# A planned layer kernel: row-tile loads planned longer, and the next block's norm roots formed beside the streams and spread through DRAM

## The chip, the cores and the metric

The kernel runs on one core of a Trainium2 chip. The metric is the device time of one execution in microseconds (us); the times shown for the kernel before are from three runs. The engines are named as in the profile: PE (TensorE, with PEld for its weight loads), DVE (VectorE), ACT (ScalarE), POOL (GpSimd) and SP (SyncE, which here only issues transfers). ScalarE issues some transfers too; that queue is written ACTq.

## The reference

One decoder layer on x of 2048 rows by 1024 columns, float32. In short:

```
h = x * rsqrt(mean(x*x, axis=-1) + 1e-6) * norm_g
p = h @ w_in                       # 7552 columns, split into three branches and gates
y_a = rwkv7(p_r, p_k, p_v, p_w, p_a) * silu(z_a)      # recurrence, 8 heads x 64
y_b = sliding_window_attention(p_q, p_sk, p_sv) * silu(z_b)   # window 128, rotary, sinks
y_c = cross_attention(p_xq, mem) * silu(z_c)          # 4 heads x 128, 256 memory rows
merged = sum over i of sigmoid(gate_i) * (y_i @ w_proj_i)
out = x + merged @ w_out
```

What the change touches is the first line: every row of x has one factor, the root of its mean square to the power -1/2. The kernel needs h transposed (channels on partitions, rows of x along the free axis), so the 512 factors of a block must stand in a tile of 128 x 512 in which all partitions hold the same row.

## The kernel before, in words

**Blocks.** The 2048 rows are worked in four blocks of 512 (`for sb in range(nsb)`, L1400). The block's h lies in SBUF as two tiles `hH`, `hL` of 128 x 8 x 512: each float32 value is split into a high part in a shorter format and the rest. A product of two such pairs takes three matmuls (high-high, high-low, low-high: L534, L535, L536 in `gemm3`). Weights come from DRAM, are split by ScalarE and VectorE (L515, L516) into tiles `whl` and put back to DRAM once (`k`, L520); later blocks fetch the split pair (L511).

**Streams.** Within a block, two generators are woven: `stream_r` prepares and runs the recurrence in 8 chunk steps (`rwkv_chain`), `stream_f` does cross attention, window attention, merges and gates. Each `yield` is an estimate of its work in us, `PACE` scales it, and `weave` always advances the generator whose clock is lowest. That gives the program order. A third generator, `x_sums` (L1354), sums the squares of the next block's x: eight times it yields 45, loads a 128 x 512 piece of x on ACTq into the one tile `sx` (L1360), and squares it on ScalarE with a running sum into `ss` (L1362).

**The end of a block.** When all streams are through, the recurrence's outputs are split, `rope_tables(sb + 1)` builds the next rotary tables (a load of the positions, spread to all partitions, then VectorE), and `x_scales` (L1364) makes the factors: VectorE adds the two halves of `ss` (L1370), GpSimd scales and takes the power -1/2 (`rpow`, L489 and L491), giving `rs` of 128 x 4. Then `bcast_T` spreads them: VectorE repeats each column 128 times (L572), TensorE transposes four 128 x 128 tiles into a PSUM tile `as_` (L574), and ScalarE copies that into `rb` (L1375). Next comes `merge(0, ...)`, which adds the first branch into the accumulators (L1321, L1322, L1328), then `x_cols` (L1378): eight loads of x transposed on ACTq (L1384), each multiplied by `rb` on VectorE (L1387) and split into `hH` (L1389, ScalarE) and `hL` (L1390, VectorE). Last, `output` multiplies by `w_out` (L1338 to L1340) and adds x (L1345).

**Row tiles.** `tmp()` and `rt_()` take tiles named `rt` from a ring of six. The temporaries of the rotary tables, the repeated roots, `rb` and the `xt` pieces all come from it, in program order.

**The planner.** The program order is not what the engines run. `steps` gives each instruction a rank (its place in the program, moved for some kinds), and `lay_out` simulates all engines: at each moment an engine takes, of the instructions that are ready by its clock, the one with the lowest rank. Tiles of a ring are opened in program order. The order found is then fixed for each engine (`order`). Engines run in that order whatever the real times are: an instruction that is not ready holds all that stand behind it on its engine. Costs are in `cost_PE` and so on. For a transfer the planner adds:

```
self.dur, self.busy = 4200 if parked else 2200, 420          # L144, ns
self.late = 5000 if any(r[0].startswith("sx") for r in self.writes) else 0
...
wires = s.end = max(wires, s.end) + s.bytes / 380
s.end += s.late
```

So a load of 256 KB counts 2.2 us and 0.69 us; the `sx` loads count 5 us more.

Of the kernel before, what the change touches and what calls it, by code (L numbers as in the profile page):

```python
# [9 lines left out]
F32 = mybir.dt.float32  # L10
# [10 lines left out]
TB = 512  # L21
# [30 lines left out]

LAT = {"PE": 200, "DVE": 45, "ACT": 35, "POOL": 80, "SP": 30}
NAMES = {mybir.EngineType.PE: "PE", mybir.EngineType.DVE: "DVE", mybir.EngineType.Activation: "ACT",
         mybir.EngineType.Pool: "POOL", mybir.EngineType.SP: "SP"}
# [2 lines left out]
class Step:  # L60


    def __init__(self, ins, masks):
        self.ins, self.eng = ins, NAMES[ins.engine]
        self.reads, self.writes = ([self.region(a.bass_ap, masks) for a in aps if getattr(a, "bass_ap", None) is not None]
                                   for aps in (ins.ins, ins.outs))
        self.reads, self.writes = ([r for r in l if r] for l in (self.reads, self.writes))
        self.before, self.after, self.opens, self.group, self.end, self.next = set(), [], [], [], None, None
        self.lat = LAT[self.eng]
        self.chain = self.eng == "PE" and any(r[0].startswith(("Zt", "W_", "R_")) or r[0] in ("W", "R") for r in self.reads)  # L70
        if self.eng == "PE":
            self.lat = 600
        outs = [a.bass_ap for l in (ins.outs, ins.ins) for a in l if getattr(a, "bass_ap", None) is not None]
        rows = [a.offset // math.prod(list(a.tensor.shape)[1:]) for a in outs[:1] + [a.bass_ap for a in ins.ins if getattr(a, "bass_ap", None) is not None]]
        self.rows = rows[0], max(rows)
        self.bytes = 512 * self.n((self.writes + self.reads)[0]) if self.is_dma() else 0
        getattr(self, "cost_" + ("SP" if self.bytes else self.eng))()

    def is_dma(self):
# [62 lines left out]
    def cost_SP(self):  # L142
        parked = any(r[0].startswith(("fq", "fb", "fv", "fn", "fy")) for r in self.reads + self.writes)
        self.dur, self.busy = 4200 if parked else 2200, 420  # L144
        self.late = 5000 if any(r[0].startswith("sx") for r in self.writes) else 0


def steps(instructions, manual, groups, follow, ahead=1000):

    out, masks, seen, byname, opener = [], {}, {}, {}, {}  # L150
    for ins in instructions:
        if isinstance(ins, mybir.BassTilePoolBoundary):
            continue
        s = Step(ins, masks)
        for rs, w in ((s.reads, False), (s.writes, True)):
            for name, parts, words, _, psum, _ in rs:
                s.before |= {q for q, w2, p2, m2 in seen.get(name, ()) if (w or w2 or psum) and q is not s and p2 & parts and m2 & words}
        for name, parts, words, *_ in s.reads:
            seen.setdefault(name, []).append((s, False, parts, words))
        for name, parts, words, *_ in s.writes:  # L160
            old = seen.setdefault(name, [])
            old[:] = [x for x in old if x[0] is s or x[2] & ~parts or x[3] & ~words] + [(s, True, parts, words)]
        s.before |= {byname[x] for x in manual.get(ins.name, ())}
        s.before |= {opener.setdefault(r[0], s) for r in s.writes + s.reads} - {s}
        for b in s.before:
            b.after.append(s)
        byname[ins.name] = s
        s.rank = len(out)
        if any(r[0].startswith(("whl", "raw")) and (s.bytes or r[5] == F32R) for r in s.writes):
            s.rank = max(s.rank - ahead, min(s.rank, FRONT))  # L170
        if s.eng != "PE" and any(r[4] for r in s.reads):
            s.rank -= 600 + 1000 * any(r[0].startswith("mm_") for r in s.reads)
        if s.eng == "DVE" and s.writes and s.writes[0][0].startswith(("ibc", "Yi")):
            s.rank += 500
        out.append(s)
    for a, b in follow.items():
        byname[a].next = byname[b]
    for names in groups:
        group = [byname[n] for n in names]
        group[0].group = group[1:]  # L180
        needs = set().union(*(s.before for s in group)) - set(group)
        for s in group:
            for b in needs - s.before:
                b.after.append(s)
            s.before |= needs
    return out
# [132 lines left out]
def build(tc, A, nsb=4):  # L319
# [30 lines left out]
    def s_ps():  # L350
        return ps.tile([128, 512], F32, name="as_", bufs=2)
# [1002 lines left out]
    def x_sums(sb, ss):  # L1354

        for i in range(4):
            for u in range(2):
                yield 45
                xr = gp_.tile([128, 512], F32, name="sx", bufs=1)
                load = nc.scalar.dma_start(xr, A["x"][sb * TB + i * 128:sb * TB + (i + 1) * 128, u * 512:(u + 1) * 512])  # L1360
                manual[load.ins.name] = [newest[0]]
                S.activation(xr, xr, AF.Square, accum_out=ss[:, i, u:u + 1])  # L1362

    def x_scales(sb, ss=None):  # L1364

        if not sb:
            rs = row_sums(x0)
        else:
            rs = xp.tile([128, 4], F32, name="rs", bufs=2)
            V.tensor_tensor(rs, ss[:, :, 0], ss[:, :, 1], op=ALU.add)  # L1370
        rpow(rs, rs, EPS, 1.0 / D)
        bc = s_ps()
        bcast_T(bc, rs, 1, 4)
        rb = tmp()
        S.activation(rb, bc, AF.Copy)  # L1375
        return rb
# [23 lines left out]
    for sb in range(nsb):  # L1400
        wa = proj(B_WA, hT)
        low = shift(wa, B_WA, pcol("mu_wa"), dcol("omu_wa"), sb, "rr_")
        S.activation(low[EV], low[EV], AF.Tanh)

        lwla = [rp.tile([128, TB], F32R, name=f"lwla{i}") for i in range(2)]
        for t, h, o in zip(lwla, (EV, OD), (OD, EV)):
            S.activation(t[h], low[h], AF.Copy)
            V.tensor_tensor(t[o], low[h], t[h].bitcast(F32), op=ALU.subtract)
        yas = []
        ya, yb, yc_ = ([], []), ([], []), ([], [])  # L1410
        accs = []

        def stream_r():
            parks = park(sb)
            dk = xp.tile([128, 4, NC_], F32, name="dk", bufs=1)
            Pl = xp.tile([128, 4, NC_], F32, name="Pl", bufs=1)
            yts = []
            for p0 in (0, 2):
                group = []
                fn, fy = (dp.tile([4, 2, NC_, 32, 32], F32, name=f"{n}{sb}_{p0}") for n in ("fn", "fy"))  # L1420
                for p in (p0, p0 + 1):
                    yield from rwkv_prep(p, p - p0, parks, dk, Pl, fn, sb, hT, lwla, group)
                yield from rwkv_inverse(group, parks, fn, fy)
                yts += [g[2] for g in group]
            yield from rwkv_chain(parks, dk, Pl, hT, yts, yas)
            yield 0.412

        def stream_f():
            for h in range(4):
                yield from cross_head(h, sb, hT, *yc_)  # L1430
            if not sb:
                rope_tables(0)
            yield from swa_kv(sb, hT)
            yield 6.938
            for j in range(4):
                yield from weave(swa_pair(j, sb, hT, *yb), merge(2, *yc_, accs, hT, first=True, orange=(2 * j, 2 * j + 1)))
            yield from merge(1, *yb, accs, hT)
            for o in range(8):
                gates.append(gate(0, o, hT))
                yield 5.908  # L1440

        gates = []
        ss = xp.tile([128, 4, 2], F32, name="ss", bufs=2)
        streams = [paced(g, PACE[min(sb, 1)][i]) for i, g in enumerate((stream_r(), stream_f()))]
        if sb + 1 < nsb:
            streams.append(x_sums(sb + 1, ss))
        for _ in weave(*streams):
            pass
        for p in range(4):
            split_y(yas[p], *ya, "a", p, sb)  # L1450
        rb = None
        if sb + 1 < nsb:
            rope_tables(sb + 1)
            rb = x_scales(sb + 1, ss)
        parts = []
        for o in range(8):
            for _ in merge(0, *ya, accs, hT, gates=gates, orange=(o,)):
                pass
            parts.append(split_acc(accs[o]))
        if rb is not None:  # L1460
            hT = x_cols(sb + 1, rb)
        output(sb, *zip(*parts))
# [4 lines left out]
def paced(g, paces):  # L1467

    for f, d in zip(paces, g):
        yield f * d  # L1470
# [83 lines left out]
```

## Time and profile before

| | |
|---|---|
| median of three runs | 2141.29 us (2141.21 to 2143.42) |
| profiled execution | 2142.16 us, its span 2140.3 us |
| granted TensorE clock | 1.0 |
| ACT busy | 803.4 us of the span |
| POOL busy | 140.5 us |
| moved by DMA | 519.17 MB, mean 243 GB/s |
| first and last issue of the 24 `sx` loads | 103.5 and 1550.5 us |

How to read it: the profile is one execution, recorded by the hardware. A row of the timeline has the start in us from the span's start, the duration in us, engine, line, operation, the tile written and the tiles read, the shape, and in brackets how long the engine had been idle and what ended that. A row of a group has the count and, for one tile, the durations of the shortest, the median and the longest in ns. Matmuls are pipelined, so that their spans overlap, and what one costs is read from the starts. The ends of the blocks, where the change works, lie at about 500 to 580, 1000 to 1090 and 1520 to 1610 us. The last block has no next x.

### The profile page before, as it was taken

The numbers are of one execution on the slowest core, as the hardware profiler recorded it, in microseconds if no ns is written. First come the engines' busy times: TensorE is split into PE (matmuls) and PEld (weight loads), VectorE is DVE, ScalarE is ACT, GpSimd is POOL, SyncE is SP. The second block draws the span as 40 slices with busy tenths as digits, with TensorE's granted clock in tenths as the row PEclk, the third lists the DMA queues.
The fourth block names the chain that finished last, engine by engine and source line by source line (L and its number), as shares of the span: only waits on it lengthen the run. The fifth ranks groups of instructions, "written<-read, shape, count | busy, mean of one in ns | idle before, by whom it ended". The sixth has DMA issues, their size and how long they took to land.

```text
span 2140.3 us, 37430 instructions
## 1 busy us (share of the span) xinstructions
PE 2124.0 (99%) x14248; PEld 1750.1 (82%) x14248; DVE 1429.2 (67%) x3246; ACT 803.4 (38%) x1699; POOL 140.5 (7%) x180
## 2 busy tenths in 40 slices
PE   9999999999999999999999999999999999999999
PEld 7888788778888888878788888887888888888787
DVE  7879888568477777546647778736455777873532
ACT  7655555335343343313424434410423334331220
POOL 1001000001001000001001000000100010000000
PEclk9999999999999999999999999999999999999999
DMA  9987898988876678695877667877676666768665
GB/s 333 361 284 266 275 300 273 348 297 263 277 213 200 189 218 233 199 313 189 278 255 216 199 178 229 235 235 256 214 265 215 210 196 203 230 188 273 209 207 180
DMA packets 308594, 519.17 MB, mean 243 GB/s; under 512 B 89280, under 2 KB 175552, under 8 KB 308416
## 3 DMA queue, kind: packets, MB, share of 16 engines
q1 hardware_dynamic: 292288, 487.42, 71.4%
q10 hardware_dynamic: 16128, 29.37, 4.2%
q8 instruction: 113, 1.85, 0.4%
q14 instruction: 65, 0.53, 0.1%
HBM read 378.80 MB, written 137.89 MB: 241 GB/s over the span
## 4 chain that ended last, share of the span: by engine, by line
PE 90%; DVE 4%; DMA 3%; issue 1%; ACT 1%; SPq 0%; POOL 0%; ACTq 0%; DVEq 0%
PE mm L535 22%; PE mm L534 22%; PE mm L536 22%; PE mm L1338 1%; PE mm L1340 1%; PE mm L1339 1%; PE rw L999 1%; PE rw L1016 1%; PE oo L1287 1%; PE rw L831 1%; DVE whl L516 1%; PE rw L850 1%; PE oo L831 1%; DMA raw<-in_w_in 1%; PE rw L921 0%
## 5 line engine op out<-in xcount | busy, mean ns | idle before, releaser
L534 PE MATMUL mm<-hH,whl 128*128 128x512 f32 x1888 | 743.6, 394 | 0.4 <-DVE carry L742 0.4
L535 PE MATMUL mm<-hL,whl 128*128 128x512 f32 x1888 | 743.7, 394 | 0.2 <-DVE hL L1390 0.2
L536 PE MATMUL mm<-hH,whl 128*128 128x512 f32 x1888 | 742.1, 393 | 0.0
L534 PEld LDWEIGHTS mm<-hH,whl 128*128 128x128 f32 x1888 | 354.8, 188 | 71.3 <-ACT big L851 0.7
L535 PEld LDWEIGHTS mm<-hL,whl 128*128 128x128 f32 x1888 | 354.9, 188 | 71.2 <-DVE hL L1390 0.6
L536 PEld LDWEIGHTS mm<-hH,whl 128*128 128x128 f32 x1888 | 354.8, 188 | 70.8
L515 ACT ACTIVATE whl<-raw 128x512 fp32r<-128x512 f32 x174 | 108.9, 628 | 124.8 <-PE mm L536 85.4
L516 DVE TENSOR_TENSOR whl<-raw,whl 128x512 fp32r<-128x512 f32 x174 | 119.9, 691 | 50.2 <-ACT whl L515 48.2
L534 PE MATMUL mm<-yh,whl 128*128 128x512 f32 x384 | 151.0, 393 | 0.1
L535 PE MATMUL mm<-yl,whl 128*128 128x512 f32 x384 | 150.2, 391 | 0.0
L536 PE MATMUL mm<-yh,whl 128*128 128x512 f32 x384 | 150.2, 391 | 0.0
L1306 ACT ACTIVATE gt<-mm 128x512 f32<-128x512 f32 x64 | 38.0, 593 | 216.7 <-PE mm L536 216.5
L534 PEld LDWEIGHTS mm<-yh,whl 128*128 128x128 f32 x384 | 72.1, 188 | 15.7 <-ACT gt L1306 0.5
L535 PEld LDWEIGHTS mm<-yl,whl 128*128 128x128 f32 x384 | 72.1, 188 | 14.9 <-DVE yl L1065 0.3
L536 PEld LDWEIGHTS mm<-yh,whl 128*128 128x128 f32 x384 | 72.1, 188 | 14.8
L1321 DVE SCALAR_TENSOR_TENSOR gt<-gt,mm 128x512 f32<-128x512 f32 x32 | 22.0, 687 | 92.3 <-PE mm L536 92.1
L487 POOL TENSOR_SCALAR st<-st 128x4 f32<-128x4 f32 (+1 forms) x32 | 12.5, 391 | 1004.9 <-DVE st L1219 407.4
L1345 DVE SCALAR_TENSOR_TENSOR ya<-mm,ya 128x512 f32<-128x512 f32 x16 | 11.0, 689 | 94.7 <-PE mm L1340 94.7
L1255 ACT ACTIVATE g<-g,mxs,st 128x128 f32<-128x128 f32 x128 | 61.6, 483 | 26.6 <-DVE mxs L1248 26.6
L892 DVE TENSOR_TENSOR ibc<-km,Yi 128x126 f32<-128x126 f32 (+22 forms) x248 | 62.8, 253 | 6.2 <-DMA km<-fn 0.6
L893 DVE TENSOR_TENSOR Yi<-Yi,ibc 128x126 f32<-128x126 f32 (+22 forms) x248 | 62.9, 254 | 5.5
L491 POOL TENSOR_TENSOR st<-st,mhalf 128x8 f32<-128x8 f32 (+1 forms) x36 | 56.2, 1562 | 3.0
(1807 smaller groups left out, 3586.0 us busy)
## 6 DMA issues: line engine op xcount, KB each, us to landing
whl<-k SPq DMA_DIRECT2D x474, 512.0 KB, 4.1
k<-whl SPq DMA_DIRECT2D x162, 512.0 KB, 4.7
raw<-in_w_in SPq DMA_DIRECT2D x118, 256.0 KB, 4.1
fq<-big SPq DMA_DIRECT2D x64, 256.0 KB, 4.5
fb<-big SPq DMA_DIRECT2D x64, 256.0 KB, 4.7
big<-fq SPq DMA_DIRECT2D x32, 512.0 KB, 6.4
big<-fb SPq DMA_DIRECT2D x32, 512.0 KB, 5.6
ya<-in_x ACTq DMA_DIRECT2D x32, 256.0 KB, 5.5
```

The source lines that it names most:

```text
L491: G.tensor_tensor(out, out, mhalf[:, :n], op=ALU.pow)
L515: S.activation(w[:, 0], raw, AF.Copy)
L516: V.tensor_tensor(w[:, 1], raw, w[:, 0].bitcast(F32), op=ALU.subtract)
L534: PE.matmul(out, lh, rh, start=i == 0, stop=False)
L535: PE.matmul(out, lh, rl, start=False, stop=False)
L536: newest[0] = PE.matmul(out, ll, rh, start=False, stop=i == n - 1).ins.name
L831: m = PE.matmul(g[:, c], BK[h, c0 + c], Q[h, c0 + c], start=True, stop=True)
L892: V.tensor_tensor(bc[:, :m, :w], Nb[:, s, s + 1:].unsqueeze(1).to_broadcast([128, m, w]), B[:, :m, s:s + 1].to_broadcast([128, m, w]), op= ...
L893: V.tensor_tensor(B[:, :m, s + 1:], B[:, :m, s + 1:], bc[:, :m, :w], op=ALU.add)
L1255: S.activation(P_, P_, AF.Exp, scale=r2[:, b, i:i + 1], bias=mx[:, b, i:i + 1], accum_out=mx[:, b, 2 + i:3 + i])
L1306: S.activation(t, gp, AF.Tanh, scale=0.5)
L1321: V.scalar_tensor_tensor(g, g, 1.0, pp, op0=ALU.add, op1=ALU.mult)
```

## The change

1. A table `LATE` gives extra landing time by the first letters of the written tile's name: `sx` 5000 ns as before, `rt` 3500 (new), `xr` 6000 (new). It is set to 0 for steps with a rank under 3000.
2. `x_sums` yields 36 in place of 45.
3. `x_scales` is called at the end of a third stream, `stream_x`, right after the sums, and not after all the streams.
4. For blocks after the first, `x_scales` no longer spreads the roots by transposes. It writes `rs` (128 x 4) to a DRAM row `xr` of 512 values with a DMA on SP; its elements go out one by one, since the row runs along the partitions. After the rope tables a second DMA on SP reads that row into all 128 partitions of `rb`. The first block's roots are spread as before.

```diff
+LATE = {"sx": 5000, "rt": 3500, "xr": 6000}
...
+        self.late = next((t for n, t in LATE.items() for r in self.writes if r[0].startswith(n)), 0)
...
-        self.late = 5000 if any(r[0].startswith("sx") for r in self.writes) else 0
...
         s.rank = len(out)
+        if s.rank < 3000:
+            s.late = 0
...
-                yield 45
+                yield 36
                 xr = gp_.tile([128, 512], F32, name="sx", bufs=1)
...
         rpow(rs, rs, EPS, 1.0 / D)
+        if sb:
+            row = dp.tile([1, TB], F32, name=f"xr{sb}")
+            nc.sync.dma_start(row[0].rearrange("(i t) -> t i", t=128), rs)
+            return row
         bc = s_ps()
...
+        rows = []
+
+        def stream_x():
+            yield from x_sums(sb + 1, ss)
+            rows.append(x_scales(sb + 1, ss))
+
         if sb + 1 < nsb:
-            streams.append(x_sums(sb + 1, ss))
+            streams.append(stream_x())
...
             rope_tables(sb + 1)
-            rb = x_scales(sb + 1, ss)
+            rb = tmp()
+            nc.sync.dma_start(rb, rows[0].to_broadcast([128, TB]))
```

## The prediction

> **What bounds the kernel now.** I read the page first: its span and the engines' shares.
>
> ```profile
> span 2140.3 us, 37430 instructions
> PE 2124.0 (99%) x14248; PEld 1750.1 (82%) x14248; DVE 1429.2 (67%) x3246; ACT 803.4 (38%) x1699; POOL 140.5 (7%) x180
> ```
>
> TensorE sets the time. Busy spans of pipelined matmuls overlap, so I took the beat from the starts in the timeline. At the end of block 0 (TensorE's rows) it is this:
>
> ```profile
> 518.76 0.39 PE L534 MATMUL mm<-yh,whl 128*128 128x512 f32 x1
> 518.99 0.39 PE L535 MATMUL mm<-yl,whl 128*128 128x512 f32 x1
> 519.21 0.39 PE L536 MATMUL mm<-yh,whl 128*128 128x512 f32 x1
> 519.88 0.66 PE L574 MATMUL as__5914<-c_ident,rt 128*128 128x128 f32 x4 [0.28 <-DVE rt L572]
> 520.29 0.47 PE L534 MATMUL mm<-yh,whl 128*128 128x512 f32 x1
> 520.61 0.39 PE L535 MATMUL mm<-yl,whl 128*128 128x512 f32 x1
> ```
>
> A 128x512 matmul that lasts 0.39 us is followed by the next after 0.22 to 0.23 us. I take 0.23 for the beat; what is longer than that between two starts is lost or is other work. Only two things can shorten the run: TensorE instructions that go, and beats that are missed. Everything on VectorE, ScalarE, GpSimd and the queues counts only where it makes a beat late. So I looked for the beats that are missed where the change works, at the ends of blocks, and next for what it may spoil elsewhere.
>
> **Removed: the spreading on TensorE.** At the end of blocks 0, 1 and 2 the old `x_scales` repeats the roots over 512 columns on VectorE (L572), transposes four 128x128 tiles (L574) and copies them out on ScalarE (L1375). The other two ends, again TensorE's rows:
>
> ```profile
> 1040.69 0.39 PE L535 MATMUL mm<-yl,whl 128*128 128x512 f32 x1
> 1040.92 0.60 PE L574 MATMUL as__11183<-c_ident,rt 128*128 128x128 f32 x4
> 1041.27 0.48 PE L536 MATMUL mm<-yh,whl 128*128 128x512 f32 x1
> 1041.59 0.40 PE L534 MATMUL mm<-yh,whl 128*128 128x512 f32 x1
> ...
> 1562.98 0.39 PE L536 MATMUL mm<-yh,whl 128*128 128x512 f32 x1
> 1563.21 0.60 PE L574 MATMUL as__16416<-c_ident,rt 128*128 128x128 f32 x4
> 1563.56 0.48 PE L534 MATMUL mm<-yh,whl 128*128 128x512 f32 x1
> 1563.88 0.39 PE L535 MATMUL mm<-yl,whl 128*128 128x512 f32 x1
> ```
>
> In block 0 the three starts 519.21, 520.29, 520.61 span 1.40 us where two beats take 0.46: 0.94 us lost, the wait of 0.28 for L572 within it. In block 1, 1040.69 to 1041.59 is 0.90, so 0.44 lost; in block 2, 1562.98 to 1563.88 is 0.90, again 0.44. Together 1.82 us, which go with certainty, because no instruction of TensorE takes their place. The copies of VectorE and ScalarE that go as well I count at nothing: at these places the matmuls beside them keep their beat.
>
> **Planned longer: loads into row tiles.** The planner (`lay_out`) fixes each engine's order with 2.2 us plus bytes/380 for such a load, 2.2 + 0.69 = 2.9 us for 256 KB. The change adds 3.5 us for tiles named `rt`, so 6.4 us. What loads take, from the DMA issues, issue to landing (the last two rows for what comes below):
>
> ```profile
> rt<-in_xt ACTq DMA_DIRECT2D x24, 256.0 KB, 5.5
> rt<-in_positions SPq DMA_DIRECT2D x4, 256.0 KB, 4.2
> fn<-big SPq DMA_DIRECT2D x64, 32.0 KB, 4.0
> c_bones<-in_bones SPq DMA_DIRECT2D x1, 1.0 KB, 5.0
> ```
>
> 5.5 us against a plan of 2.9: VectorE comes to the product with `xt` (L1387) too early and, being in order, holds what stands behind it. At the end of block 1 that reaches TensorE. Timeline, from the ACT queue's, VectorE's and TensorE's rows:
>
> ```profile
> 1043.48 0.45 ACTq L1384 DMA_DIRECT2D rt<-in_xt  x1
> ...
> 1049.16 0.69 DVE L1387 TENSOR_TENSOR rt<-rt 128x512 f32<-128x512 f32 x1 [2.63 <-DMA rt<-in_xt]
> ...
> 1048.89 0.39 PE L536 MATMUL mm<-yh,whl 128*128 128x512 f32 x1
> 1050.56 0.47 PE L1338 MATMUL mm<-whl,g 128*128 128x512 f32 x1 [1.28 <-issue]
> ...
> 1052.02 0.39 PE L1338 MATMUL as__11425<-whl,g 128*128 128x512 f32 x1
> 1052.91 0.50 PE L1338 MATMUL mm<-whl,g 128*128 128x512 f32 x1 [0.50 <-DVE g L1321]
> ```
>
> The load issued at 1043.48 lands 5.7 us later; VectorE stands 2.63 us, and the merge's products (L1321), which the output matmuls need, stand behind it. TensorE loses 1050.56 - 1048.89 - 0.23 = 1.44 and 1052.91 - 1052.02 - 0.23 = 0.66, in all 2.10 us. Planned at 6.4, the product comes after the landing of 5.7, and VectorE does its merges first. What is late next there: nothing that I see, since VectorE is then only as far behind as its own work. I take 2.10; the bounds are 0 (the wait moves to another load) and 2.10.
>
> **Moved: sums and roots into the streams.** With a step of 36 in place of 45 the eighth piece of x is due at 8 x 36 = 288 of the weave's clock, not 360; the front stream's yields sum to 256, which its pace of 1.35 makes 346, and the recurrence's to 195 x 1.2 + 90 x 0.8 = 306. So the last squares, the sum (L1370), two GpSimd instructions (L489, L491) and the row write come near the end of the chunk steps, and not behind both streams. The broadcast read follows the rope tables, on SP. First and last of these instructions:
>
> ```profile
> L1370 DVE TENSOR_TENSOR rs<-ss x3: 156/156/157, 516.9 to 1560.0; 128x4 f32<-128x4 f32 x3
> L491 POOL TENSOR_TENSOR rs<-rs,mhalf x4: 1007/1009/1015, 19.4 to 1560.5; 128x4 f32<-128x4 f32 x4
> L1387 DVE TENSOR_TENSOR rt<-rt x24: 682/685/694, 534.6 to 1581.7; 128x512 f32<-128x512 f32 x24
> ```
>
> Block 0 sums at 516.9 and first multiplies by the roots at 534.6. A row write costs between 4.0 and 5.0 us by the rows above (32 KB in 128-byte pieces, 1 KB in 8-byte pieces; I take 5.0, the nearer form), and the broadcast read is the same form and size as that of the positions, 4.2. That is 9.2 us, half of the 17.7 even at the old place, and the new place is 72 units of the weave's clock earlier (a unit is the kernel's own estimate of a us). I count it at nothing; without that cover, had the roots stayed behind the streams in a block where the first product follows at once, it would be up to 9.2 us on VectorE. The read's 256 KB, three times, is 0.8 MB of 519 MB moved: nothing.
>
> **The waits that this adds.** SP's queue gets the row write, which waits for GpSimd, and ahead of the next x the broadcast read; behind them stand chunk fetches and weights. ScalarE gets two squares per block earlier. And one thing lies in the code alone: the extra time now holds only for steps of rank 3000 and up, so the `sx` loads early in block 0, planned at 2.9 + 5.0 until now, are planned at 2.9. Counted in the program of before, block 0's streams hold the steps 460 to some 4,500, and the weave's clock is at 180 near step 2,500 and at 225 near step 3,100. So five of the eight loads (36 to 180) lie under rank 3000, and the sixth (216) at its edge. What those take, from the answers on `sx` for five windows around the first five loads:
>
> ```profile
> DMA to landing us min/median/max: 5.1/5.1/5.1
> DMA to landing us min/median/max: 5.0/5.0/5.0
> DMA to landing us min/median/max: 4.2/4.2/4.2
> DMA to landing us min/median/max: 3.7/3.7/3.7
> DMA to landing us min/median/max: 3.4/3.4/3.4
> ```
>
> The excess over 2.9 is 2.2 + 2.1 + 1.3 + 0.8 + 0.5 = 6.9 us that ScalarE may stand behind a square. Bounds for TensorE: 0 and 6.9. I take 0, since 220 to 320 us, where TensorE is shortest of work, is VectorE's stretch and not ScalarE's:
>
> ```profile
> 220.00:320.00 100.00, 96.75 (x686) 80.52 (x685) 83.94 (x167) 55.35 (x126) 6.69 (x9) 1.00 0.87 289
> ```
>
> (columns: PE, PEld, DVE, ACT, POOL busy.) ScalarE is free 45 of these 100 us.
>
> **The sum.** 1.82 + 2.10 = 3.92 us off. The profiled execution took 2142.16 us around its span of 2140.3, 0.9 above the median of the runs, 2141.29; it becomes 2138.2, and the median 2137.4. A measurement of this kernel can tell about 0.2% (4.3 us) from no change, so the forecast lies just inside "same", at -0.18%.
>
> **Rivals.**
> *More goes than that.* Every order is planned anew from the first moved square on, and the waits of block 0 may go with it. The window above has 3.25 us of TensorE idle, all behind VectorE; a plan that deals it differently could save them: 2137.4 - 3.25 = 2134.1. For it: long waits elsewhere are so few that most places are evidently dealt without any. Against it: nothing in the change lightens VectorE there, and a new plan can as well make a new gap.
> *The stall of block 1 only moves.* Then the transposes alone count: 2141.29 - 1.82 = 2139.5. For it: landings of the `xt` loads (L1384) reach 8.2 us, over the 6.4 of the plan:
>
> ```profile
> DMA to landing us min/median/max: 3.3/5.5/8.2
> ```
>
> *ScalarE is held in block 0* (the other side). If the squares' 6.9 us pass whole to TensorE: 2137.4 + 6.9 = 2144.3, slower than before. It decides from 3.92 / 6.9 = 57% passed on; at the 6.2 us that the slowest of all `sx` loads takes it is 5 x 3.3 = 16.5 us and 24%:
>
> ```profile
> DMA to landing us min/median/max: 2.6/4.6/6.2
> ```
>
> Against it: ScalarE's free share, and TensorE's order holds weights prepared ahead.
> *SP is held by the row write.* It stands for GpSimd's power (1.0 us, the row of L491 above) if that comes late, and for its own issue. The nearest issues, scatters in short rows:
>
> ```profile
> L873 SPq DMA_DIRECT2D fv<-rt x64: 577/598/1647, 102.4 to 1882.2; - x64
> PE rw L999 <- DMA Zt<-fv: 0.6, 1, 0.6
> PE rw L1008 <- DMA big<-fb: 0.5, 1, 0.5
> ```
>
> With 0.6 to 1.65 us for the issue it is 1.6 to 2.65 us a block, 4.8 to 8.0 in three, if none is absorbed: 2142.2 to 2145.4. For it: the chunk steps already wait for two fetches (the last two rows, from the waits of TensorE). Against it: only two, of 64 and 32.
> [...] No row here shows a write in 4-byte pieces of this size.
>
> **How the numbers follow.** Forecast (2137.4, spread of 1.5 either way by the two terms and small gaps) 0.40; more goes 0.25; the stall moves 0.13; ScalarE held 0.16; SP held 0.06. The bound for faster is 2137.0, 0.4 under the forecast: of its 0.40 I put 0.18 below and 0.22 above. Faster 0.18 + 0.25 = 0.43. Slower (over 2145.6) is half of the two last, 0.11. Same is the rest, 0.46. The range: below, the case with more going and the two fetch waits of 1.1 us with it, 2133.0; above, most of the held cases, 2145.5. It leaves out about 0.05 below and 0.12 above.
>
> **What would show it.** Right: no L574 at the ends of blocks; L1387 without a wait on a DMA, and L1338 in its beat there; L1370 some tens of us before the ends; the squares (L1362 now) never awaited by others. Wrong: ScalarE idle before the squares in the first 300 us with TensorE gaps behind; SP standing at the row write with Zt or big awaited; or new gaps on TensorE in places that the change doesn't touch, which would mean that the new order, not its parts, sets the result.

## The result and the profile after

The changed kernel takes 2150.36 us (median of 6 runs, 2146.52 to 2153.77) where the kernel before takes 2141.76 in the same comparison: a ratio of 1.0036, 95% interval 1.0026 to 1.0046. It is slower by 8.6 us by the medians, and lies above the range of the prediction. The profiled execution took 2148.24 us.

The page after, the same two rows as before:

```profile
span 2146.4 us, 37434 instructions
PE 2125.1 (99%) x14236; PEld 1751.5 (82%) x14236; DVE 1426.8 (66%) x3243; ACT 804.3 (37%) x1698; POOL 136.1 (6%) x180
```

The twelve transposes are gone (14248 - 14236), as announced. TensorE's busy time says nothing of the loss. The waits of TensorE from 400 to 520 us do; first before, then after (whom it waited for, us in total, times, longest):

```profile
PE rw L1008 <- DMA big<-fb: 0.5, 1, 0.5
PE as__5914 L574 <- DVE rt L572: 0.3, 1, 0.3
PE rw L1008 <- DVE W L1001: 0.2, 1, 0.2
```

```profile
PE rw L1002 <- DMA Zt<-fv: 6.5, 1, 6.5
PE rw L1019 <- DVE Zt L1017: 1.2, 1, 1.2
PE mm L537 <- ACT g L1309: 0.6, 1, 0.6
PE rw L1011 <- DMA big<-fb: 0.4, 1, 0.4
```

One wait of 6.5 us on a chunk fetch is new (line numbers behind the first lines of the change are 3 higher after, and 7 higher behind `x_scales`). The timeline of SP and TensorE after, around it, shows what stands ahead of that fetch on the queue:

```profile
447.64 0.55 SPq L1377 DMA_DIRECT2D xr<-rs  x1
448.28 2.07 SPq L946 DMA_DIRECT2D Zt<-fv  x2
...
454.62 0.33 PE L1002 MATMUL rw<-Zt,big 128*64 128x64 f32 x2
461.44 0.37 PE L1002 MATMUL rw<-Zt,big 128*64 128x64 f32 x2 [6.49 <-DMA Zt<-fv]
```

The row write of the new roots, 2 KB, stands first, then the two halves of `Zt`; TensorE goes on as the second half lands (issued at 449.8, 11.6 us). The landings of the row write in its windows in blocks 0, 1 and 2, and of the first `Zt` fetch (issue to landing, us; each answer holds one transfer):

```profile
DMA to landing us min/median/max: 13.3/13.3/13.3
DMA to landing us min/median/max: 11.3/11.3/11.3
DMA to landing us min/median/max: 11.6/11.6/11.6
DMA to landing us min/median/max: 12.9/12.9/12.9
```

Before, the median of these fetches was 5.2 us over the whole run, and 6.6 (4.4 to 9.4) in the last chunk steps of block 0. The wait has a second price. The stretches during and after it (PE, PEld, DVE, ACT, POOL busy, granted clock, DMA share, GB/s):

```profile
455.00:461.00 6.00, 0.00 (x0) 0.00 (x0) 0.18 (x1) 0.00 (x0) 0.00 (x0) 0.83 0.86 160
461.00:466.00 5.00, 4.56 (x66) 4.07 (x67) 1.41 (x5) 0.00 (x0) 0.61 (x1) 0.52 0.85 314
466.00:472.00 6.00, 5.92 (x94) 4.46 (x94) 4.00 (x10) 1.12 (x2) 0.00 (x0) 1.00 0.50 166
```

Some 4 us into the wait, near 459 us, TensorE's clock fell to half, and it stayed there until near 466: in single microseconds the column reads 0.97 from 458 to 459, 0.50 in each of the six from 459 to 465, 0.62 in the next and 1.00 from 466. TensorE worked from 461.4, so some 4.5 us ran at half speed: about 2.2 us more (an estimate from the clock column, not measured alone).

Block 2 shows the write by itself, since nothing critical stands behind it there. Here are stretches of two us after its issue at 1502.38:

```profile
1502.00:1504.00 2.00, 2.00 (x17) 1.62 (x10) 1.78 (x4) 1.09 (x2) 0.36 (x1) 1.00 0.15 9
1504.00:1506.00 2.00, 2.00 (x10) 1.68 (x9) 1.91 (x8) 0.63 (x1) 0.00 (x0) 1.00 0.10 33
...
1510.00:1512.00 2.00, 2.00 (x13) 1.69 (x12) 0.10 (x1) 1.40 (x3) 0.00 (x0) 1.00 0.20 20
1512.00:1514.00 2.00, 2.00 (x10) 1.64 (x9) 1.62 (x3) 1.51 (x3) 1.24 (x2) 1.00 0.65 51
1514.00:1516.00 2.00, 2.00 (x10) 1.68 (x9) 1.79 (x4) 0.63 (x1) 1.13 (x1) 1.00 0.84 340
```

Until the write had landed the core moved 9 to 51 GB/s, and 340 the moment after. It did not lack requests: SP issued weight loads of 512 KB at 1503.96 and 1506.7, and so on. The first of them, and below it the same load of experiment e1, which has the same order and a write in 128 pieces:

```profile
DMA to landing us min/median/max: 11.8/11.8/11.8
DMA to landing us min/median/max: 3.8/3.8/3.8
```

The share of DMA (the last column but one) is 0.10 to 0.65 in that time, so on their mean the DMA engines were not full of work; what the loads stood behind is not shown. TensorE lost nothing here. That is the theory the experiments were made for: **this 2 KB write in 512 pieces all but stops the transfers for some 10 us, and what it costs depends on what stands behind it.** The rivals: the new order itself asks for the fetch too late; the hold is in SP's queue alone; or ScalarE is held in block 0.

### The profile page after: what moved, and what is told of

Same layout as the page of the kernel before. It is cut to its first block, busy times and chain, and to the rows that moved or that the text cites. A ratio compares the mean times of both kernels' runs of the same rounds, so it can differ in the third digit from the quotient of the medians.

```text
span 2146.4 us, 37434 instructions
## 1 busy us (share of the span) xinstructions
PE 2125.1 (99%) x14236; PEld 1751.5 (82%) x14236; DVE 1426.8 (66%) x3243; ACT 804.3 (37%) x1698; POOL 136.1 (6%) x180
## 2 busy tenths in 40 slices
DMA packets 310610, 519.96 MB, mean 242 GB/s; under 512 B 90912, under 2 KB 177184, under 8 KB 310432
## 4 chain that ended last, share of the span: by engine, by line
PE 88%; DVE 4%; DMA 4%; ACT 2%; issue 1%; SPq 0%; POOL 0%; DVEq 0%; ACTq 0%; POOLq 0%
PE mm L537 22%; PE mm L538 22%; PE mm L539 22%; PE mm L1341 1%; PE mm L1342 1%; PE mm L1343 1%; DVE whl L519 1%; DMA Zt<-fv 1%; PE oo L1290 1%; PE rw L1019 1%; PE rw L834 1%; PE rw L1002 1%; DMA raw<-in_w_in 1%; PE rw L853 1%; PE oo L834 1%
```

## The experiments

**e1: the same order, fewer pieces.** The row is laid out so that a partition's four roots are neighbours.

```diff
-            nc.sync.dma_start(row[0].rearrange("(i t) -> t i", t=128), rs)
+            nc.sync.dma_start(row[0].rearrange("(t i) -> t i", i=4), rs)
```

> The changed kernel with the row write laid out so that each partition sends its 4 roots as one piece of 16 bytes: 128 pieces in place of 512 of 4 bytes. The order of every engine and queue is the changed kernel's, instruction by instruction. It leaves out the right order of the roots in the row (each row of x of blocks 1 to 3 gets another row's root). Theory W (the write in 512 pieces holds the transfers issued around it; in block 0 these are chunk fetches): the write lands in about 5 us and not 13.3, the fetch behind it in 5 to 6 and not 12.9, the 6.5 us wait of TensorE goes, and with it the 6.8 us at clock 0.50 behind it (about 2.2 us more): 2139.5 to 2141.7 us. Rival R (the new order as such asks for the fetches too late, or the queue is full there anyway): fetch and wait stay above 10 and 5 us, 2148 to 2150. Between them, if the cost goes with the number of pieces: the write lands in 7 us, the wait shrinks to about 1 us and the clock stays at 1.00.

Measured: 2140.81 us, ratio to before 1.0001 (0.9992 to 1.0010), 9.5 us under the changed kernel's median. The row write's landings in blocks 0 and 2, and the first `Zt` fetch behind it:

```profile
DMA to landing us min/median/max: 8.0/8.0/8.0
DMA to landing us min/median/max: 1.6/1.6/1.6
DMA to landing us min/median/max: 7.2/7.2/7.2
```

TensorE's longest wait on `Zt` is 0.8 us, and the clock is 1.0 in the profiled execution. With the same order on every engine, only the pieces differ; so they are the cause of these 9.5 us, and the order is not. In block 0 the write still took 8.0 us, more than the 5 I expected; around its place the DMA share is high (1.06 from 440 to 455 us in the changed kernel).

**e9: between the two.** 256 pieces of 8 bytes, again in the same order.

```diff
+            nc.sync.dma_start(row[0].rearrange("(a t i) -> t a i", a=2, i=2), rs.rearrange("p (a i) -> p a i", i=2))
```

> The changed kernel, order the same instruction by instruction, with the row write in 256 pieces of 8 bytes (512 of 4 in the changed kernel, 128 of 16 in e1). It leaves out the right order of the roots in the row. If the hold goes with the number of pieces (11.6 us at 512 and 1.6 at 128 in block 2, about 26 ns a piece): the write in block 2 lands in about 5 us, in block 0 in 9 to 10; the wait of TensorE on the chunk fetch is 1.5 to 4 us; 2143 to 2146. If there is a threshold between 4 and 8 bytes: as e1, 2140 to 2141. If any piece under 16 bytes does it: as the changed kernel, 2148 to 2151.

Measured: 2143.91 us, ratio 1.0010 (0.9999 to 1.0021); TensorE's longest wait on `Zt` is 2.7 us. The write's landings in blocks 0 and 2:

```profile
DMA to landing us min/median/max: 9.8/9.8/9.8
DMA to landing us min/median/max: 4.1/4.1/4.1
```

The pieces are in the trace: it counts 90912 packets under 512 bytes with 512 pieces, 90144 with 256 and 89760 with 128, which is 3 x 256 and 3 x 384 fewer for the three writes. In block 2 the landings are 1.6, 4.1 and 11.6 us for 128, 256 and 512 pieces: 20 ns for each piece added at first and 29 ns then, with no sharp threshold among the three. Whether it is the number of pieces or their size that counts, these three cannot tell, since both change.

**e7: another queue.** The row write is issued by ScalarE.

```diff
-            nc.sync.dma_start(row[0].rearrange("(i t) -> t i", t=128), rs)
+            nc.scalar.dma_start(row[0].rearrange("(i t) -> t i", t=128), rs)
```

> The changed kernel with the row write (512 pieces) issued on ScalarE's queue, some 1 to 2 us from its old place; SP's queue no longer holds it. If the hold is in SP's queue (order of completion): chunk fetches in 5 to 7 us, no wait of over 2 us, 2140 to 2143. If the pieces stop the DMA engines for all queues (theory W as block 2 of the changed kernel suggests, where the moved bytes fell to 9 to 51 GB/s for 11 us): fetches issued within 5 us of the write still take 10 us and more, wait of 4 to 7 us and the halved clock again, 2147 to 2151.

Measured: 2151.14 us, ratio 1.0041 (1.0026 to 1.0055). The waits of TensorE:

```profile
PE rw L1002 <- DMA Zt<-fv: 7.9, 2, 6.7
```

The write went out at 447.3 on ScalarE's queue. SP issued a fetch of `big` at 448.81 and the first half of `Zt` at 449.23; their landings:

```profile
DMA to landing us min/median/max: 10.6/10.6/10.6
DMA to landing us min/median/max: 10.4/10.4/10.4
```

In block 2 SP's first three weight loads behind the write took 11.6, 10.1 and 8.6 us, where e1 has 3.8, 3.4 and 3.2. So here transfers of SP were held beside a write that was not in SP's queue, and the order of one queue does not explain it. What held them, the runs do not show. TensorE's 6.7 us come about a little otherwise than in the changed kernel, though. They end with the second half of `Zt`, which SP issued only at 459.91 and which took 4.0 us; SP itself had stood, by what the profile names as the end of that wait, until the row write landed:

```profile
SPq L944 <- DMA xr<-rs: 9.7, 1, 9.7
```

**e4 and e5: another place.** In e4 the write is emitted behind the streams.

```diff
         if sb:
-            row = dp.tile([1, TB], F32, name=f"xr{sb}")
-            nc.sync.dma_start(row[0].rearrange("(i t) -> t i", t=128), rs)
-            return row
+            return rs
...
+            row = dp.tile([1, TB], F32, name=f"xr{sb}")
+            nc.sync.dma_start(row[0].rearrange("(i t) -> t i", t=128), rows[0])
             rope_tables(sb + 1)
```

> The changed kernel with the row write (still 512 pieces of 4 bytes) issued behind the streams, just ahead of the rope tables, where weights stand behind it and no chunk fetch. Theory W: the write still lands in 11 to 13 us and the weights behind it in 7 to 12, but up to seven tiles of weights are ahead, so that TensorE waits under 1.5 us a block for it: 2139 to 2144. If the next x waits for the roots (11.6 + 5.6 us of write and read), up to 3 us more in a block. Rival R: if the position in the chunk steps doesn't matter, 2148 to 2150 as the changed kernel.

Measured: 2149.15 us, ratio 1.0035 (1.0023 to 1.0048). It tests nothing that I meant it to: the planner takes what is ready, and issued the write at 447.7 us again, among the chunk fetches, with a wait of 6.0 us. Emitting the write later in the program did not move it here. In e5 the write truly stands behind, because the sums do (step 45; the rest is e3, below):

```diff
+        if sb:
+            row = dp.tile([1, TB], F32, name=f"xr{sb}")
+            nc.sync.dma_start(row[0].rearrange("(i t) -> t i", t=128), rs)
+            rb = tmp()
+            nc.sync.dma_start(rb, row.to_broadcast([128, TB]))
+            return rb
```

> The kernel before with the longer plan (as e3) and the row write in 512 pieces and the broadcast read in place of the transposes, but sums and roots where they were, behind the streams: the write now really stands there, among weights, by its dependence. Theory W (the write all but stops the transfers for about 10 us wherever it stands; what that costs is set by what is queued behind it): the write lands in about 11 us, weights right behind it in 8 to 12; seven weight tiles of 2.7 us each cover most: no wait of over 3 us from it, 2135.5 (no transposes, nothing else) to 2143 (block 0 and 1, where weights come as raw pieces with only three buffers, wait up to 3 us each). If the cost is the same anywhere: 2137.5 - 1.3 + 8.7 = 2145 or more.

Measured: 2150.65 us, ratio 1.0042 (1.0027 to 1.0057); not the 2135.5 to 2143 that I expected of the theory, but what I had put down for a cost that is the same anywhere. The writes landed in 11.0, 8.8 and 11.2 us. Two waits of TensorE, in blocks 0 and 2:

```profile
PE mm L1341 <- DVE g L1324: 9.5, 2, 4.9
```

VectorE is not the cause. It stood waiting for ScalarE, and ScalarE's waits just before are these, of block 0 and of block 2:

```profile
ACT whl L518 <- DMA raw<-in_w_out: 6.9, 1, 6.9
ACT g L1329 <- DMA rt<-in_xt: 8.0, 1, 8.0
```

In block 0 ScalarE stands at a raw weight that landed 11.5 us after its issue, in block 2 behind its own loads of x. The cover of seven weight tiles that I relied on did not help, since ScalarE, in its fixed order, held what stood behind the one load that was late (6.9 and 8.0 us). So the cost is about the same at either place, by other waits.

**e3: the longer plan alone.** The kernel before with `LATE` (`sx` 5000, `rt` 3500, 0 under rank 3000) and nothing else.

> The kernel before with the longer plan for rt tiles alone (3.5 us more, none for ranks under 3000, as the change has it); sums, roots and spread as before. Prediction's term: the stall of 2.1 us at the end of block 1 goes, 2139.2. Prediction's rival: squares planned 5 us earlier in block 0 hold ScalarE, up to 6.9 us more, 2146. Theory W says neither more nor less than the first: within 3 us of 2139.2, no wait on a chunk fetch of over 1 us.

Measured: 2137.51 us, ratio 0.9979 (0.9971 to 0.9988): faster by 3.7 us by the medians of that comparison (2141.21 before). The stall at the end of block 1 is gone.

**e8: the longer plan, with the `sx` loads of block 0 still planned late.**

```diff
-        if s.rank < 3000:
+        if s.rank < 3000 and not any(r[0].startswith("sx") for r in s.writes):
             s.late = 0
```

> The kernel before with the longer plan as in e3, but with the sx loads of block 0 still planned 5 us longer below rank 3000 (the rt loads not). It tests the prediction's rival that ScalarE is held by squares planned too early: if that costs, it is up to 6.9 us faster than e3, 2131 to 2136. If ScalarE's hold is absorbed: e3 within its spread, 2136 to 2139.

Measured: 2139.84 us, ratio 0.9988 (0.9979 to 0.9996), 1.8 us under the 2141.65 of before in that comparison. It is not faster than e3 but 2.3 us slower by the medians (the intervals overlap a little), so planning these loads early shows no cost; the prediction's rival of a held ScalarE is refuted. The trace of the changed kernel agrees: from 60 to 520 us ScalarE stood once before a square for a load into `sx`, for 0.5 us. Two of TensorE's longest waits in e8:

```profile
PE rw L853 <- DVE big L849: 1.0, 1, 1.0
PE oo L1290 <- DVE g L1278: 0.9, 1, 0.9
```

They stand near 265 us, as in the kernel before, and e3 has neither. So e8 holds the term of block 1 alone, and these two waits of block 0, 1.9 us, fit e3's other 2 us.

**e2, e6 and e11: moving the sums.** e2 has everything of the change but spreads by the old transposes. e6 is e3 with the step of 36 alone. e11 is e6 with 45 in block 0.

```diff
-            rb = tmp()
-            nc.sync.dma_start(rb, rows[0].to_broadcast([128, TB]))
+            rb = x_spread(rows[0])          # e2: bc, bcast_T and the copy of before
...
-                yield 45
+                yield 36                         # e6
...
-                yield 36
+                yield 45 if sb == 1 else 36      # e11 (sb is the next block)
```

> The changed kernel with sums and roots formed in the streams and the loads planned longer, but the roots spread as before, by four transposes at the end of each block; no row write and no broadcast read. Theory W: no wait of over 2 us on a chunk fetch, clock 1.00 throughout; against the kernel before, the 2.1 us stall of block 1 gone and the transposes (0.44 us each without a wait) kept: about 2139.5, 2138 to 2142. Rival R (moving sums and roots into the streams, or the longer plan, is what spoils block 0): still over 2146.

> The kernel before with the longer plan (as e3) and the step of 36 in x_sums; roots formed and spread at the old place by transposes. It splits the 4.2 us that e2 took over e3. If the earlier x loads and squares in the chunk steps of block 0 cost it: 2141 to 2143. If the roots in the streams (two GpSimd instructions and the sum) or the chance of a new order cost it: 2137 to 2139.

> e6 with the step of 36 in blocks 1 and 2 alone; in block 0 it is 45, as in e3. e6 took 5.4 us more than e3 by the medians, and its added waits of TensorE stand in block 0 (1.6 us at 345 us, 0.4 and 1.0 at 443 and 458, 1.35 at 510). If those are the cost: 2137 to 2139, as e3. If the step costs in every block, or by the chance of a new order: 2140 to 2143.

Measured: e2 2141.69 (ratio 1.0003, 0.9994 to 1.0011), e6 2142.89 (1.0003, 0.9993 to 1.0012), e11 2138.11 (0.9982, 0.9972 to 0.9991). So the step of 36 in block 0 takes back what the longer plan gives (e6 is 5.4 us over e3 by the medians, some 5 by the ratios); the roots' place in the streams adds nothing measurable to it. TensorE's waits from 340 to 520 us, e6 and then e11:

```profile
PE as__4109 L1272 <- DVE g L1268: 1.6, 1, 1.6
PE rw L1011 <- DMA big<-fb: 1.6, 1, 1.6
PE mm L537 <- ACT g L1309: 1.4, 1, 1.4
PE rw L1002 <- DMA Zt<-fv: 1.0, 1, 1.0
PE rw L1019 <- DVE Zt L1017: 0.4, 1, 0.4
```

```profile
PE rw L1011 <- DMA big<-fb: 1.3, 1, 1.3
PE mm L537 <- issue: 0.6, 1, 0.6
PE rw L1011 <- DVE W L1004: 0.2, 1, 0.2
```

That is 6.0 against 2.1 us. Why these five waits come with the step, through the x loads among the fetches or only through another deal of the same work, was not taken apart further.

**e10: a better version.** e5 with the row of e1, made right by reading the spread roots with a stride:

```diff
-            nc.sync.dma_start(row[0].rearrange("(i t) -> t i", t=128), rs)
+            nc.sync.dma_start(row[0].rearrange("(t i) -> t i", i=4), rs)
...
+                xi = xt.rearrange("p (i t) -> p i t", i=4)
+                V.tensor_tensor(xi, xi, rb.rearrange("p (t i) -> p i t", i=4), op=ALU.mult)
```

> The kernel before with the longer plan, step 45, and the roots spread by row write and broadcast read behind the streams as in e5, but the row holds the four roots of a partition side by side (128 pieces of 16 bytes), and the products with xt read the spread roots with a stride of four, so that each row of x gets its own root. Theory W: the write lands in 2 to 5 us, no wait of over 2 us of TensorE for what stands behind it (4.6 and 4.9 in e5), no transposes: 2135 to 2138.5, so at or under e3 (2137.5), and under the kernel before. If it is the broadcast read or the order of e5 that cost: 2147 or more.

Measured: 2138.88 us, ratio 0.9984 (0.9975 to 0.9993), 11.8 us under e5, and just over the 2135 to 2138.5 expected: the row through DRAM is no fault in itself. It does not beat e3, which with no such row at all is the fastest kernel here.

The way from the kernel before to the changed one, step by step and by the medians: longer plan -3.7 (e3), step of 36 +5.4 (e6 over e3), roots in the streams -1.2 (e2 under e6), spreading through DRAM in place of the transposes -0.9 (e1 under e2), and 512 pieces in place of 128 +9.5 (the changed kernel over e1). Each step starts where the last one ended, so that their sum, +9.1, has to come out near the measured +8.6 and proves nothing; the 0.5 is the difference of two medians of the kernel before. The third and fourth are within what the intervals leave open.

## Why the prediction was wrong

*TensorE bounds the kernel, and only late beats count*: right. So did the loss come, most of the 9.5 us over e1 as one late chunk fetch and the slow clock behind it.

*Transposes, -1.82 us*: the instructions went; e1 under e2 shows -0.9, not told apart from nothing or from 1.8.

*Longer plan, -2.10 us*: right in mechanism for the stall of block 1 (e8 has no wait of TensorE there), and in size as far as the interval tells (e8, -1.8; 0.9 to 4.5 off by its ratio). The whole part gives -3.7, since the squares planned earlier in block 0, which I had feared, dealt that block's work anew, and two of its waits are gone.

*Moved sums, nothing*: wrong too. I costed each moved instruction's own time and its cover, and not what the new step does to the plan of block 0, where its loads and squares come at other moments. It is +5.4 (e6 over e3), all of it in block 0 (e11); by which of the five waits and why stays open.

*The row write, "I count it at nothing"*: this is the step that failed. I asked when the roots are needed, which was safe (the first product came long after), and what the write takes, from transfers of 1 KB and 32 KB (5.0 and 4.0 us). It took 11.3 to 13.3. I never asked what the write does to the transfers beside it. No row before showed a 4-byte scatter to DRAM, and I bounded only its duration by the nearest rows, not its effect on others; the 9 to 51 GB/s of block 2 are that effect, and 9.5 us are its price (the changed kernel over e1). That is the most of the 12.5 us between the change that I forecast (3.9 us off) and the measured one (8.6 us more).

*The rival that SP is held*: the right place (a chunk fetch late, TensorE at the chunk steps), the wrong mechanism. Its price was one queue's issue, 1.6 to 2.65 us in each of three blocks; the issue took 0.55 us at most (SP's row of L1377), the order within the queue was not what held (e7), and one block paid 6.5 us and the halved clock. I had counted the short pieces as issue time only. By the packet counts a write in 512 pieces has 384 packets more than one in 128 (beside e9), and the cost lay in the transfers (11.6 us to landing against 1.6 in block 2) and not in the issue.

*ScalarE held in block 0*: refuted by e8.

The halved clock was in no part of the prediction: 0.83 on the mean of the wait of 6.5 us, and 0.52 in the 5 us behind it. So this wait cost more than its length; e3 shows a slower clock after a shorter one too (last section).

## What to carry to other kernels

Cost a small transfer by its pieces, and cost it to its neighbours: here 2 KB in 512 pieces took 11 to 13 us, and weight and chunk fetches behind it took 11.6 to 12.9. Laying the row so that each partition sends one piece, and undoing the order in the reader's stride, took that away (e10: the writes landed in 2.2 to 3.0 us), for products that are longer on VectorE (below). When a change has several parts, time them apart: here the longer plan alone was worth 3.7 us, and the rest lost 12.

## What the runs showed of the hardware

A scatter of 4-byte pieces to DRAM took 11.6 us in block 2, 8-byte pieces 4.1 and 16-byte pieces 1.6, for the same 2 KB; the core moved 9 to 51 GB/s during the first, and transfers on the other issuing queue were held as well (in e7 SP's loads took 10.4 and 11.6 us with the write on ScalarE's queue). A wait much shorter than 6.5 us was once followed by a slower clock too. Behind e3's longest wait in mid-run, 1.7 us on a chunk fetch between 410 and 415 us, stands this (clock 0.66 on the mean):

```profile
415.00:420.00 5.00, 5.00 (x44) 3.52 (x44) 3.33 (x8) 0.63 (x1) 0.00 (x0) 0.66 1.01 388
```

It did not always come: in e6, with two waits of 1.6 us within 340 to 520 us, the clock is 1.00 on the mean of 340 to 420 and of 420 to 520 us. What decides was not tried.

And with a stride of four elements in one operand VectorE's product of 128x512 float32 took 1074 ns in e10, where it took 685 in the kernel before without it:

```profile
L1398 DVE TENSOR_TENSOR rt<-rt x24: 1057/1074/1109, 535.8 to 1589.4; 128x512 f32<-128x512 f32 x24
```
